# Level scores of an HGRN2 chunk: full-width matmuls replaced by matmuls at the array's four quadrants

## The chip, the cores and the metric

One NeuronCore of one Trainium2 chip. The metric is device time in microseconds of one execution of the whole layer; smaller is better. A core has TensorE (matmuls, with a separate stream of weight loads), VectorE, ScalarE, GpSimd (POOL in the profile) and SyncE (SP, which issues most transfers); each works through its own list of instructions in order and waits where data are missing.

## What is computed

One layer of a hybrid decoder for 256 tokens of width 2048: one wide input projection, three token mixers (a gated linear recurrence, a sliding-window attention, a short convolution), projections, a gated merge, an output projection and a layer norm. The change touches the recurrence alone, whose intra-chunk scores are

```
b = cumsum(log f)                               # per head and channel
diff = b[t] - b[s]
decay = exp(where(causal, diff, -inf))
scores[t, s] = sum_k q[t, k] * k[s, k] * decay[t, s, k]
out[t] = sum_s scores[t, s] * v[s]
```

There are 8 heads with 128 channels each.

## The kernel before

The large matrix products (input projection, branch projections, output projection) take nearly all the time. They are `gemm` calls: weights come in granules of 1 MB (`load_granule`), and each half of a granule is split by `split_w` into a rounded part `hi` (ScalarE, L111) and a rest `lo` (VectorE, L112), so that products in a short float format keep float32 accuracy. `rows` (L140 to L142) and `columns` (L147 to L150) issue the matmuls into one of four `acc` banks. `total` (L188, L189) and others empty the banks. Four buffers each of `hi` and `lo` let the splits run ahead of TensorE.

The recurrence, the attention and the transposes run in the shadow of these products. They are generators in the list `tasks`: after each half granule `gemm` calls `pump()`, which runs the first task up to its next `yield`. So TensorE's list holds the main products with small groups of the tasks' matmuls in between. A scheduler of the framework then fixes the order of instructions on each engine, by its own priorities.

`hgrn(hf, ...)` handles four heads; it runs twice (`hf` 0 and 1). It doesn't form the decay for each pair of tokens. It works in levels h = 1, 2, 4, ..., 128: at level h, the 256 tokens fall into blocks of 2h, and the scores of the upper half of a block (queries) against its lower half (keys) are one product, with the decay split at the boundary between the halves. For each level VectorE and ScalarE make `qc` (queries times `eu`, L346 and L348) and `kk`, a buffer of `kp` (keys times `el`, L347 and L350; two buffers in turn), and carry the prefix and suffix sums on (L352, L353, in `PS`). A product then goes into a PSUM bank `lev`, and its valid part into `st`, which holds the scores of four heads and two chunks of 128 tokens, keys on partitions.

- Levels 1 and 2 use VectorE products summed by a matmul with ones (`near`).
- Levels 4, 8 and 16: for each of 4 heads and 2 chunks one float32 matmul (L385) with 128 key columns as weights against 64 query columns. This gives the scores of all 128 keys with all 64 upper-half queries, of which only the blocks on the diagonal are wanted. One `copy_predicated` on VectorE (L389) moves those into `st`, chosen by a byte mask that stands in `C["mask"]` from column `FAR` on, 64 columns a level.
- Levels 32 and 64 compute only the diagonal blocks (L375), with weights of h columns at partitions 2hi to 2hi + h of the output, and ScalarE copies them (L380). At level 32 these are two places, output partitions 0 to 31 and 64 to 95; at level 64 one.
- Level 128 is one matmul a head (L392, copy L395).

After the levels come the products with the values (L405, L406), the norm and the transposes.

The float32 matmuls of the levels show two records each in the profile, and two weight loads.

Of the kernel before, what the change touches and what calls it, by code (L numbers as in the profile page):

```python
# [16 lines left out]
P = 128  # L17
# [15 lines left out]
EYE, NEAR, FAR, MASKS = 0, {1: 128, 2: 192}, 320, 512  # L33
# [15 lines left out]
def hybrid_kernel(ctx, tc, a, out):  # L49
    nc = tc.nc  # L50
# [16 lines left out]
    def t4(shape, name, dt=F32):  # L67
        return w4.tile(shape, dt, tag="w4", name=name)

    def t2(shape, name, dt=F32):  # L70
        return w4.tile(shape, dt, tag="w2", name=name, bufs=W2)

    def bank(name):
        return bgp.tile([P, NC], F32, tag="bg", name=name)
# [207 lines left out]
    def hgrn(hf, fk, q, v, gate):  # L282
# [20 lines left out]
        def near(e, dst, mask):  # L303

            hi, lo = t2([P, 512], "nh", F32R), t2([P, 512], "nl", F32R)
            nc.scalar.copy(out=hi, in_=e)
            nc.vector.tensor_sub(out=lo, in0=e, in1=f32(hi))
            yield
            ps = bank("near")
            nc.tensor.matmul(out=ps, lhsT=C["ones"], rhs=hi, start=True, stop=False)  # L310
            nc.tensor.matmul(out=ps, lhsT=C["ones"], rhs=lo, start=False, stop=True)
            r = mask.shape[-1]
            nc.vector.copy_predicated(out=dst, mask=mask, data=ps.rearrange("p (x b r) -> p x b r", x=dst.shape[1], r=r))
# [9 lines left out]
        for n, h in enumerate((1, 2, 4, 8, 16, 32, 64, 128)):  # L323
            nb = T // (2 * h)

            def halves(x, h=h):
                y = x.rearrange("p h t -> p (h t)").rearrange("p (b two r) -> p b two r", two=2, r=h)
                return y[:, :, 0], y[:, :, 1]

            qlo, qup = halves(q)  # L330
            klo, kup = halves(k)
            plo, pup = halves(pre)
            slo, sup = halves(suf)
            flo, fup = halves(f)
            qc = t2([P, 4, P], "qc")
            qv = qc.rearrange("p h t -> p (h t)").rearrange("p (b r) -> p b r", r=h)
            kk = kp[:, n % 2]
            if h == 1:
                nc.vector.tensor_mul(out=qv, in0=qup, in1=fup)
                kv = klo  # L340
            else:
                eu = t2([P, 512], "eu")
                el = t2([P, 512], "el")
                euv = eu.rearrange("p (b r) -> p b r", r=h)
                elv = el.rearrange("p (b r) -> p b r", r=h)
                nc.scalar.activation(out=euv, in_=pup, func=AF.Exp)  # L346
                nc.scalar.activation(out=elv, in_=slo, func=AF.Exp)  # L347
                nc.vector.tensor_mul(out=qv, in0=qup, in1=euv)  # L348
                kv = elv if h == 2 else halves(kk)[0]
                nc.vector.tensor_mul(out=kv, in0=klo, in1=elv)  # L350
            if h < 128:
                nc.vector.tensor_add(out=slo, in0=slo, in1=pup[:, :, h - 1 : h].to_broadcast([P, 4 * nb, h]))  # L352
                nc.vector.tensor_add(out=pup, in0=pup, in1=plo[:, :, h - 1 : h].to_broadcast([P, 4 * nb, h]))  # L353
            yield
            if h < 128:
                b = 64 // h
                dst = st.rearrange("p h t (b two r) -> p (h t) b two r", two=2, r=h)[:, :, :, 1]
            if h <= 2:
                for j in range(h):
                    e = t2([P, 512], "e")  # L360
                    nc.vector.tensor_mul(out=e.rearrange("p (b r) -> p b r", r=h), in0=qv,
                                         in1=kv[:, :, j : j + 1].to_broadcast([P, 4 * nb, h]))
                    yield from near(e, dst, C["mask"][:, NEAR[h] + 64 * j : NEAR[h] + 64 * j + 64]
                         .rearrange("p (a b r) -> p a b r", a=1, r=h).to_broadcast([P, 8, b, h]))
                    yield
                continue
            ps = bank("lev")
            if 32 <= h < 128:

                for hd in range(4):  # L370
                    for t in range(2):
                        for i in range(b):
                            s_ = slice(2 * h * i, 2 * h * i + h)
                            o = (2 * hd + t) * h
                            nc.tensor.matmul(out=ps[s_, o : o + h],  # L375
                                             lhsT=kk[:, hd, t * P + s_.start : t * P + s_.stop],
                                             rhs=qc[:, hd, t * 64 + i * h : t * 64 + i * h + h], start=True, stop=True)
                for i in range(b):
                    s_ = slice(2 * h * i, 2 * h * i + h)
                    nc.scalar.copy(out=dst[s_, :, i], in_=ps[s_, : 8 * h].rearrange("p (x r) -> p x r", x=8))  # L380
            elif h < 128:
                for hd in range(4):
                    for t in range(2):
                        o = (2 * hd + t) * 64
                        nc.tensor.matmul(out=ps[:, o : o + 64], lhsT=kk[:, hd, t * P : t * P + P],  # L385
                                         rhs=qc[:, hd, t * 64 : t * 64 + 64], start=True, stop=True)
                m = (C["mask"][:, FAR + 64 * (n - 2) : FAR + 64 * (n - 1)]
                     .rearrange("p (a b r) -> p a b r", a=1, r=h).to_broadcast([P, 8, b, h]))
                nc.vector.copy_predicated(out=dst, mask=m, data=ps.rearrange("p (x b r) -> p x b r", x=8, r=h))  # L389
            else:  # L390
                for hd in range(4):
                    nc.tensor.matmul(out=ps[:, hd * P : hd * P + P], lhsT=kk[:, hd, 0:P], rhs=qc[:, hd],  # L392
                                     start=True, stop=True)
                s01 = t2([P, 4, P], "s01")
                nc.scalar.copy(out=s01, in_=ps.rearrange("p (h t) -> p h t", h=4))  # L395
            yield
# [3 lines left out]
        for t in range(2):  # L400
            ps = bank("pv")
# [14 lines left out]
        o = t4([P, 2, NC], "oa")  # L416
# [126 lines left out]
    C = {}  # L543
# [5 lines left out]
    ps = bank("warm")  # L549
# [4 lines left out]
    for hf in range(2):  # L554
        v = rows_out(rows512(AI + hf, None if hf else first), "va")
        q = t4([P, 4, T], "qa")
        for u in range(2):
            acc = columns256(AQ + 2 * hf + u)
            qr = t2([P, 2, T], "qr")
            for b in range(2):  # L560
                total(qr[:, b], acc[b])
            swish(q[:, 2 * u : 2 * u + 2], qr, HD**-0.5)
        if hf == 0:
            C.update(constants())
        fk = t8([P, 2, 4, T], "fk")
        for u in range(2):
            forget(hf, u, fk[:, 0, 2 * u : 2 * u + 2], columns256(AFG + 2 * hf + u))
        gate = rows_out(rows512(AG + hf), "ga", silu=True)
        nc.gpsimd.tensor_mul(out=gate, in0=gate,
                             in1=C["gn"][:, hf * NC : hf * NC + NC].rearrange("p (o n) -> p o n", o=1)  # L570
                             .to_broadcast([P, 2, NC]))
        tasks.append(hgrn(hf, fk, q, v, gate))
# [15 lines left out]
    for w in range(2):  # L588
        r = slice(64 * w, 64 * w + 64)
# [34 lines left out]
    for d in range(4):  # L624
        m = t4([P, 2, NC], "merged")
# [166 lines left out]
```

## Time and profile before

| | |
|---|---|
| three runs | 1025.15, 1025.85, 1026.55 us; median 1025.85 |
| the profiled execution | 1026.14 us, span of its instructions 1024.3 us |
| TensorE | busy 1009.3 us (99% of the span), 5214 matmul records |
| VectorE | busy 656.9 us (64%) |
| ScalarE | busy 516.8 us (50%) |
| transfers | 192.60 MB, mean 188 GB/s |

The profile is that of one execution. The table gives busy time of engines; an engine's busy share is an average over stages. The span is the time from the first to the last recorded instruction. Times inside rows are microseconds from the span's start. "PE" is TensorE's matmul stream, "PEld" its weight loads, "PEldq" and "DVEq" waits in the engines' instruction sequencers.

### The profile page before, as it was taken

To read this page: it belongs to the slowest core of one execution; us is meant where nothing else is said; L and a number is where in the kernel's file an instruction comes from. 1 tells how busy PE (TensorE), PEld (TensorE's weight loads), DVE (VectorE), ACT (ScalarE), POOL (GpSimd) and SP (SyncE) were. 2 spreads that over 40 slices of the span, in tenths; PEclk is the share of its full clock that TensorE was granted. 3 is DMA by queue.
4 is the path that set the end of the run, shared out by engine and by line. 5 is a ranking of instruction groups with operands and counts; after the bars stand their busy time and mean duration, and the time that the engine had idled before them with its cause. 6 is when DMAs were issued, how large, how long until landed. Compare 5 with 4: busy or idle time off the path is not lost.

```text
span 1024.3 us, 13046 instructions
## 1 busy us (share of the span) xinstructions
PE 1009.3 (99%) x5214; PEld 855.4 (84%) x5214; DVE 656.9 (64%) x810; ACT 516.8 (50%) x702; POOL 32.4 (3%) x32
## 2 busy tenths in 40 slices
PE   8999999999999999999999999999999999999995
PEld 5888888888988888888888888888888888888885
DVE  6557788689855777777764455545554555545666
ACT  5546577656564665646554434444444434444441
POOL 1000000210010000000000000000000000000003
PEclk9999999999999999999999999999999999999998
DMA  8655545354455545444455555555455556665442
GB/s 324 242 194 177 205 136 180 137 189 144 165 196 182 191 156 200 166 168 144 168 199 203 179 194 205 173 197 205 170 200 202 180 193 237 254 248 193 177 164 83
DMA packets 30253, 192.60 MB, mean 188 GB/s; under 512 B 3776, under 2 KB 4576, under 8 KB 8176
## 3 DMA queue, kind: packets, MB, share of 16 engines
q1 hardware_dynamic: 28368, 184.85, 50.9%
q10 hardware_dynamic: 1152, 4.72, 1.3%
q0 software_dynamic: 672, 2.20, 0.7%
q8 instruction: 41, 0.67, 0.3%
q14 instruction: 20, 0.16, 0.0%
HBM read 189.63 MB, written 2.12 MB: 187 GB/s over the span
## 4 chain that ended last, share of the span: by engine, by line
PE 97%; DMA 1%; DVE 1%; SPq 0%; ACT 0%; issue 0%
PE acc L148 24%; PE acc L142 19%; PE acc L140 19%; PE acc L141 19%; PE acc L147 11%; PE lev L385 1%; DMA raw<-in_w_rows 1%; PE sc L454 1%; PE pvb L497 1%; PE acc L150 1%; PE pT L487 1%; PE pv L406 0%; PE mT L259 0%; PE lev L375 0%; DVE xres L677 0%; DVE xres L675 0%
## 5 line engine op out<-in xcount | busy, mean ns | idle before, releaser
L112 DVE TENSOR_TENSOR lo<-raw,hi 128x1024 fp32r<-128x1024 f32 (+1 forms) x341 | 414.9, 1220 | 291.5 <-ACT hi L111 290.5
L111 ACT CAST hi<-raw 128x1024 fp32r<-128x1024 f32 (+1 forms) x341 | 356.7, 1048 | 388.2 <-PE acc L141 264.2
L148 PE MATMUL acc<-xs,hi 128*128 128x512 f32 x1056 | 371.9, 396 | 0.0
L147 PE MATMUL acc<-xs,lo 128*128 128x256 f32 x990 | 278.4, 281 | 0.0
L148 PEld LDWEIGHTS acc<-xs,hi 128*128 128x128 f32 x1056 | 197.0, 188 | 43.7
L140 PE MATMUL acc<-hi,xs 128*128 128x512 f32 (+1 forms) x544 | 210.5, 387 | 2.3 <-ACT hi L111 2.3
L142 PE MATMUL acc<-lo,xs 128*128 128x512 f32 (+1 forms) x544 | 208.4, 384 | 0.4 <-DVE lo L112 0.3
L141 PE MATMUL acc<-hi,xs 128*128 128x512 f32 (+1 forms) x544 | 208.7, 384 | 0.0
L147 PEld LDWEIGHTS acc<-xs,lo 128*128 128x128 f32 x990 | 186.8, 189 | 2.2
L140 PEld LDWEIGHTS acc<-hi,xs 128*128 128x128 f32 x544 | 102.5, 188 | 24.5 <-ACT hi L111 4.4
L142 PEld LDWEIGHTS acc<-lo,xs 128*128 128x128 f32 x544 | 102.2, 188 | 21.3 <-DVE lo L112 1.2
L141 PEld LDWEIGHTS acc<-hi,xs 128*128 128x128 f32 x544 | 102.6, 189 | 19.8
L188 ACT COPY rest<-acc 128x256 f32<-128x256 f32 x66 | 24.3, 373 | 46.2 <-PE acc L148 45.3
L140 PE MATMUL acc<-hi,m 128*128 128x512 f32 (+1 forms) x120 | 45.2, 376 | 0.0
L142 PE MATMUL acc<-lo,m 128*128 128x512 f32 (+1 forms) x120 | 45.0, 375 | 0.0
L141 PE MATMUL acc<-hi,m 128*128 128x512 f32 (+1 forms) x120 | 45.0, 375 | 0.0
L142 PEld LDWEIGHTS acc<-lo,m 128*128 128x128 f32 x120 | 22.6, 188 | 4.1
L140 PEld LDWEIGHTS acc<-hi,m 128*128 128x128 f32 x120 | 22.6, 188 | 4.0
L141 PEld LDWEIGHTS acc<-hi,m 128*128 128x128 f32 x120 | 22.6, 188 | 4.0
L140 PE MATMUL acc<-hi,oa 128*128 128x512 f32 x64 | 24.9, 389 | 0.0
L141 PE MATMUL acc<-hi,oa 128*128 128x512 f32 x64 | 24.9, 389 | 0.0
L142 PE MATMUL acc<-lo,oa 128*128 128x512 f32 x64 | 24.9, 389 | 0.0
(187 smaller groups left out, 912.1 us busy)
## 6 DMA issues: line engine op xcount, KB each, us to landing
raw<-in_w_cols SPq DMA_DIRECT2D x68, 1024.0 KB, 4.8
raw<-in_w_rows SPq DMA_DIRECT2D x60, 1024.0 KB, 4.7
raw<-in_w_out SPq DMA_DIRECT2D x16, 1024.0 KB, 4.8
raw<-in_w_proj_hgrn SPq DMA_DIRECT2D x8, 1024.0 KB, 4.7
raw<-in_w_proj_attn SPq DMA_DIRECT2D x8, 1024.0 KB, 4.7
raw<-in_w_proj_conv SPq DMA_DIRECT2D x8, 1024.0 KB, 4.7
raw<-in_w_rows SPq DMA_DIRECT2D x7, 512.0 KB, 8.9
bias<-bias_dr POOLq DMA_DIRECT2D x2, 1024.0 KB, 6.1
```

The costliest lines, as they stand in the source:

```text
L111: nc.scalar.copy(out=hi, in_=r)
L112: nc.vector.tensor_sub(out=lo, in0=r, in1=f32(hi))
L140: nc.tensor.matmul(out=acc, lhsT=xk[:, 0, ts], rhs=hi, start=first, stop=False)
L141: nc.tensor.matmul(out=acc, lhsT=xk[:, 1, ts], rhs=hi, start=False, stop=False)
L142: nc.tensor.matmul(out=acc, lhsT=xk[:, 0, ts], rhs=lo, start=False, stop=last)
L147: nc.tensor.matmul(out=acc[:, :T], lhsT=lo, rhs=xk[:, 0], start=False, stop=False)
L148: nc.tensor.matmul(out=acc, lhsT=hi, rhs=xk, start=first, stop=last)
L150: nc.tensor.matmul(out=acc[:, :T], lhsT=lo, rhs=xk[:, 0], start=False, stop=False)
L188: nc.scalar.copy(out=rest[p], in_=acc[p, T:])
L385: nc.tensor.matmul(out=ps[:, o : o + 64], lhsT=kk[:, hd, t * P : t * P + P], rhs=qc[:, hd, t * 64 : t * 64 + 64], start=True, stop=True)
L454: nc.tensor.matmul(out=ps[:, o_ : o_ + 2 * nk], lhsT=q[:, 2 * g + x, m, blk * P : blk * P + P], rhs=kz[n][:, hf, :, 0:nk], start=(i == 0), ...
L487: nc.tensor.transpose(out=ps[:, x * P : x * P + P], in_=s[:, x // 2, x % 2, j * P : j * P + P], identity=C["ident"])
```

## The change

At levels 4, 8 and 16 each 128x64 product is replaced by four products of 32 keys with 16 queries (32 weight columns, 16 moving columns), which lie on the diagonal: keys 32i to 32i + 31 of a chunk and the 16 upper-half queries of the same 32 tokens, i = 0 to 3. The contraction still runs over all 128 channels. The output of product i lies at PSUM partitions 32i to 32i + 31, and all 4 x 2 heads and chunks stand next to each other in 16 columns each, 128 columns in all. The one predicated copy of 128 partitions and 512 columns becomes four of 32 partitions and 128 columns, with the matching piece of the same mask. Arithmetic and result stay the same.

```
-                        o = (2 * hd + t) * 64
-                        nc.tensor.matmul(out=ps[:, o : o + 64], lhsT=kk[:, hd, t * P : t * P + P],
-                                         rhs=qc[:, hd, t * 64 : t * 64 + 64], start=True, stop=True)
-                m = (C["mask"][:, FAR + 64 * (n - 2) : FAR + 64 * (n - 1)]
-                     .rearrange("p (a b r) -> p a b r", a=1, r=h).to_broadcast([P, 8, b, h]))
-                nc.vector.copy_predicated(out=dst, mask=m, data=ps.rearrange("p (x b r) -> p x b r", x=8, r=h))
+                        o = (2 * hd + t) * 16
+                        for i in range(4):
+                            nc.tensor.matmul(out=ps[32 * i : 32 * i + 32, o : o + 16],
+                                             lhsT=kk[:, hd, t * P + 32 * i : t * P + 32 * i + 32],
+                                             rhs=qc[:, hd, t * 64 + 16 * i : t * 64 + 16 * i + 16],
+                                             start=True, stop=True)
+                for i in range(4):
+                    r_ = slice(32 * i, 32 * i + 32)
+                    m = (C["mask"][r_, FAR + 64 * (n - 2) + 16 * i : FAR + 64 * (n - 2) + 16 * i + 16]
+                         .rearrange("p (a b r) -> p a b r", a=1, r=h).to_broadcast([32, 8, 16 // h, h]))
+                    nc.vector.copy_predicated(out=dst[r_, :, 16 // h * i : 16 // h * (i + 1)], mask=m,
+                                              data=ps[r_, : 8 * 16].rearrange("p (x b r) -> p x b r", x=8, r=h))
```

Behind the changed place every line number of the new kernel is higher by 7 (its predicated copy is L395).

TensorE's list at level 4 of the second half (`hf` 1), inside the product of the attention's values; before:

```order
L140 MATMUL acc<-hi,xs_84 128x256
L141 MATMUL acc<-hi,xs_84 128x256
L142 MATMUL acc<-lo,xs_84 128x256
L385 MATMUL lev<-qc,kp 128x64 x8
L140 MATMUL acc<-hi,xs_85 128x256
```

and with the change:

```order
L140 MATMUL acc<-hi,xs_84 128x256
L141 MATMUL acc<-hi,xs_84 128x256
L142 MATMUL acc<-lo,xs_84 128x256
L387 MATMUL lev<-qc,kp 32x16 x32
L140 MATMUL acc<-hi,xs_85 128x256
```

Eight matmuls became 32 between the same neighbours; so it is at the other five places, and the rest of TensorE's list is as before.

VectorE's list at level 8 of the second half; L353 is the second of the two sums that the next level needs, before:

```order
L112 TENSOR_TENSOR lo<-raw,hi 128x1024
L353 TENSOR_TENSOR PS<-PS 128x32x16
L389 COPY_PREDICATED st<-mask,lev 128x64x8
L112 TENSOR_TENSOR lo<-raw,hi 128x1024
L348 TENSOR_TENSOR qc<-qa,eu 128x512
L350 TENSOR_TENSOR kp<-fk,el 128x16x32
```

and with the change:

```order
L112 TENSOR_TENSOR lo<-raw,hi 128x1024
L395 COPY_PREDICATED st<-mask,lev 32x8x2x8 x4
L353 TENSOR_TENSOR PS<-PS 128x32x16
L112 TENSOR_TENSOR lo<-raw,hi 128x1024
L588 TENSOR_TENSOR vb<-acc,vb 128x256
L348 TENSOR_TENSOR qc<-qa,eu 128x512
```

The four copies now stand ahead of L353; at level 16 of the second half they pass L353 and one split in the same way. Elsewhere a few neighbours change places.

## Rows read from the trace of the kernel before

**Rows 1.** The page: busy time, granted clock by slice, the chain that ended last.

```profile
PE 1009.3 (99%) x5214; PEld 855.4 (84%) x5214; DVE 656.9 (64%) x810; ACT 516.8 (50%) x702; POOL 32.4 (3%) x32
...
PEclk9999999999999999999999999999999999999998
...
PE 97%; DMA 1%; DVE 1%; SPq 0%; ACT 0%; issue 0%
```

**Rows 2.** Waits of TensorE: us in total, times, longest; later than 30 us none.

```profile
PE acc L140 <- ACT hi L111: 2.3, 2, 1.8
...
PE acc L142 <- DVE lo L112: 0.3, 1, 0.3
```

**Rows 3.** Line L385: durations in ns (min/median/max), first and last start, shape.

```profile
L385 PEld LDWEIGHTS lev<-qc,kp x96: 188/192/192, 147.3 to 268.3; 128*128 128x128 f32 x96
L385 PE MATMUL lev<-qc,kp x96: 217/275/275, 147.5 to 268.3; 128*128 128x64 f32 x96
```

**Rows 4.** Timeline, TensorE, level 4: start, duration in us, engine, line, operation.

```profile
146.94 0.40 PE L148 MATMUL acc<-xs,hi 128*128 128x512 f32 x1
...
147.29 0.39 PE L148 MATMUL acc<-xs,hi 128*128 128x512 f32 x1
147.52 1.89 PE L385 MATMUL lev<-qc,kp 128*128 128x64 f32 x16
...
149.42 0.40 PE L148 MATMUL acc<-xs,hi 128*128 128x512 f32 x1
```

**Rows 5.** Timeline, TensorE, level 32 with 32 weight columns at two places.

```profile
169.32 0.39 PE L148 MATMUL acc<-xs,hi 128*128 128x512 f32 x1
169.64 0.70 PE L375 MATMUL lev<-qc,kp 128*32 128x32 f32 x32
...
170.49 0.39 PE L148 MATMUL acc<-xs,hi 128*128 128x512 f32 x1
```

**Rows 6.** Line L375 by stretch: length, busy time and records begun (x), clock.

```profile
169.14:169.70 0.56, 0.06 (x3) 0.06 (x5) 1.00 0.00 0
169.14:170.12 0.98, 0.48 (x30) 0.48 (x32) 1.00 0.00 0
280.09:280.69 0.60, 0.10 (x1) 0.10 (x2) 1.00 0.00 0
280.09:281.49 1.40, 0.90 (x15) 0.90 (x16) 1.00 0.00 0
```

**Rows 7.** Timeline, TensorE, level 64 with 64 weight columns at one place.

```profile
280.27 0.39 PE L148 MATMUL acc<-xs,hi 128*128 128x512 f32 x1
280.59 1.15 PE L375 MATMUL lev<-qc,kp 128*64 128x64 f32 x16
...
281.89 0.40 PE L148 MATMUL acc<-xs,hi 128*128 128x512 f32 x1
```

**Rows 8.** Timeline, VectorE, level 4 of the second half.

```profile
253.69 0.70 DVE L389 COPY_PREDICATED st<-mask,lev 128x512 f32<-128x512 uint8 x1
254.29 2.34 DVE L112 TENSOR_TENSOR lo<-raw,hi 128x1024 fp32r<-128x1024 f32 x2
```

**Rows 9.** Timeline, VectorE, eight operations of 128 columns in a row.

```profile
195.57 2.16 DVE L420 SCALAR_TENSOR_TENSOR oa<-pv,rs,ga 128x128 f32<-128x128 f32 x8 [1.79 <-POOL rs L415]
```

**Rows 10.** A stretch of VectorE: length, busy time and instructions, clock, transfers.

```profile
224.36:259.50 35.14, 35.14 (x51) 1.00 0.40 141
```

**Rows 11.** Timeline, TensorE: first use of the split behind the copy.

```profile
256.62 0.28 PE L142 MATMUL acc<-lo,xs 128*128 128x256 f32 x1
```

**Rows 12.** Timeline, VectorE and TensorE, level 4 of the second half.

```profile
244.87 0.69 DVE L350 TENSOR_TENSOR kp<-fk,el 128x512 f32<-128x512 f32 x1
...
251.72 1.90 PE L385 MATMUL lev<-qc,kp 128*128 128x64 f32 x16
```

**Rows 13.** Line L392's wait in TensorE's sequencer, and the stretch from it to L392.

```profile
L392 PEldq EVENT_SEMAPHORE  x1: 51/51/51, 284.2 to 284.2; - x1
...
284.28:287.10 2.82, 2.82 (x18) 2.49 (x17) 1.20 (x1) 1.05 (x1) 0.00 (x0) 1.00 0.84 340
```

## Prediction

> **What bounds the kernel now.** I first read the page's busy times, its slices and its chain: TensorE is busy 99% of the span at full granted clock in all slices but the last, and the chain that ended last runs 97% through it [rows 1]. Then the waits of TensorE over the whole span: apart from its first instruction it waited 2.6 us, for hi and lo halves, all of it before 30 us [rows 2], far from the code that changes. So what shortens a TensorE instruction between 130 and 290 us shortens the kernel, unless VectorE then comes late; what VectorE gains or loses counts only through such a lateness.
>
> Next the line that changes. Six blocks (levels 4, 8, 16 in each of two halves) hold 96 matmul records and 96 weight loads, all 128 columns of weights against 64 moving columns [rows 3]: 8 matmuls per block, float32, two records each. Their price is read from the starts of the neighbours, since matmul ends overlap [rows 4]. From the L148 before the block to the L148 behind it pass 149.42 - 147.29 = 2.13 us; two neighbours without a block stand 147.29 - 146.94 = 0.35 us apart. The block costs 1.78 us, 111 ns a record. Six blocks: 10.7 us, 1% of the span.
>
> **What the new block costs.** It has 32 matmuls, so 64 records, each with 32 columns of weights, 16 moving columns and a quadrant of the output. TensorE's order keeps each block's place between the same neighbours, so nothing else moves there. The nearest rows are those of line L375 for level 32, which already uses 32-column weights at two places of the array. There 169.32 to 170.49 is 1.17 us, less the same 0.35: 0.82 us for 32 records [rows 5]. How this splits into a fixed part and a pace is read by counting the records begun up to two moments: 27 records in 0.42 us, 15.6 ns each; the 64-column weights of level 64, which all go to one place, 14 in 0.80 us, 57 ns [rows 6]. Fixed part: 0.82 - 32 x 0.0156 = 0.32 us; from level 64, whose block costs 1.62 - 0.35 = 1.27 us [rows 7], 1.27 - 16 x 0.057 = 0.36 us. I take 0.34. It is the emptying of the array on both sides of a block with narrower weights (the full-width block shows none).
>
> The pace at four places is not in the trace. *Dear end:* as at two places, 15.6 ns: 64 x 0.0156 + 0.34 = 1.34 us, 0.44 saved. *Cheap end:* the columns loaded set the pace (57 ns for 64 columns at one place, about half that for 32, and half again at 15.6 because two places work side by side), then four places halve it to 7.8 ns: 0.84 us, 0.94 saved. Neither is nearer: the form is the first one's, the number of places the other's double. I take the middle, 11.7 ns: 0.75 + 0.34 = 1.09 us, **0.69 us saved a block, 4.1 us for six**; the ends are 2.6 and 5.6 us.
>
> By the Trainium skill (TensorE: Matmul & The Clock Gate, "Part 3: Packing small matmuls — row/col tiling") matmuls at different tiles start about 4 ns apart, with which the cheap end would hold. No row here shows four places, so it moves nothing in the sum.
>
> **VectorE.** One predicated copy of 512 columns becomes four of 128 columns on 32 partitions. The old one stands 0.60 us ahead of its successor (254.29 - 253.69) [rows 8]. The nearest row for a short one is a run of eight 128-column operations out of the same kind of bank: 2.16 / 8 = 0.27 us each [rows 9]. Four cost 1.08, so 0.48 us more a level, 2.9 us in all; if the length meant nothing it would be 4 x 0.60 - 0.60 = 1.8 us more; below 0.48 only if the fixed part fell too. I take 0.48, since the column count is the same.
>
> What hides it: VectorE makes the lo halves ahead of TensorE. The tightest place I found among the six is the first block of the second half. From 224.36 to 259.50 VectorE has no idle time [rows 10], so it cannot catch up. Behind the copy there stand two lo splits, the first done at about 255.5 (half of 2.34 behind 254.29) [rows 8]; TensorE first needs it at 256.62 [rows 11]. Of this 1.1 us the copies take 0.48 and the faster block 0.69: about 0 left, hence no stall in the sum; with the dear copies and the cheap block, 1.1 - 1.8 - 0.9 = 1.6 us of stall, once. The scores' own inputs have more room: the shortest distance from a level's last product (begun 244.87, 0.69 long) to its block (251.72) is 6.2 us [rows 12].
>
> The order also moves on VectorE: in the second half, at levels 8 and 16, the copies now stand ahead of the addition L353. They wait for the block, and behind them now wait that addition, ScalarE's two exponentials for the next level and two products. The old copy of level 8 itself waited for its block, so the move delays the next level by a microsecond or two, and those 6.2 us cover it. On ScalarE a few casts change places with exponentials; TensorE reaches them later by the same cover. No DMA is added; SP and POOL keep their work. TensorE's program grows by 6 x 48 records with their loads, fetched ahead like the rest: nothing.
>
> **Sum.** The profiled execution took 1026.14 us (span 1024.3 and 1.84 around it); 1026.14 - 4.1 = 1022.0. It stands 0.3 above the median of the runs, 1025.85, so I forecast **1021.8 us**.
>
> **The rivals.**
> *A, the forecast* (0.71): the four places work side by side, 7.8 to 15.6 ns: 1020.2 to 1023.3. For it: the even pace over 32 records, and one place's 57 ns against two places' 15.6.
> *B, handing out instructions becomes the bound* (0.15). A block has 128 instructions. At L392 TensorE's sequencer had passed a wait at 284.2 whose matmul came at 287.1, with 18 matmuls and 17 loads between, edges included [rows 13], so it runs some 33 instructions ahead. The 64 of level 32 therefore had about 16 pairs in store and got 16 more within their 0.5 us, a pair in 32 ns at worst. Then 48 pairs of the new block need up to 48 x 0.032 = 1.54 us, with 0.34 together 1.88: 0.10 dearer than before, 6 x 0.1 = 0.6 us, 1026.5. Better paces give anything between that and A; I put its middle at 1024.8. Against it: the pace of level 32 doesn't slacken behind its first 16 records.
> *C, a floor under the distance of two matmuls* (0.04). With a floor of 25 ns, 64 x 0.025 + 0.34 = 1.94 us, 0.16 dearer, 1026.8. Against it: 15.6 ns [rows 6]. Such a floor, about 25 ns from start to start however small the matmul, is a rule of the Trainium skill (TensorE: Matmul & The Clock Gate, "Wait — 56ns, not 53.3ns?"); by this trace it doesn't hold for narrow weights at two places.
> *D, slower: the places do not work side by side* (0.07). Then each record costs a place's own pace, twice 15.6 = 31.2 ns: 64 x 0.0312 + 0.34 = 2.34 us, 0.56 dearer, 6 x 0.56 = 3.4 us: 1029.2. It decides from (1.78 - 0.34) / 64 = 22.5 ns a record. For it: the places beyond two are untried here, and all matmuls keep the full 128 rows. Against it: two places do run together. The Trainium skill (TensorE: Matmul & The Clock Gate, "What overlaps and what doesn't") says that weight loads overlap with matmuls under way only where the row group differs; by that rule this rival would hold, but level 32, whose row groups are all the same, disagrees with its 15.6 ns.
> *E, VectorE's lateness* (0.03): the 1.6 us stall, 4.1 - 1.6 = 2.5 us faster, 1023.3. That the change does not do what it says is excluded by the order: 32 matmuls of 32x16 stand at each of the six places.
>
> **How the numbers follow.** Runs of this kernel spread by 0.14%, so 0.2%, 2.05 us, is about what can be told. A and E are faster by more than that (0.74), as is 0.02 of B; the rest of B and C lie within (0.17); D is slower (0.07). I move 0.01 from faster to slower for a stall that I have not seen. Faster 0.75, same 0.17, slower 0.08. The range reaches from the cheap end of A (5.6 us, 1020.2, less 0.2 of spread) up through B's middle to just above no change: 1020.0 to 1026.0. A alone: 1020.2 to 1023.3.
>
> **What would show it.** Right: blocks of 64 records with the neighbours about 1.4 us apart instead of 2.13, records 8 to 15 ns apart in sixteens without slackening, TensorE's waits unchanged, VectorE about 2.9 us busier. B would show an even first quarter of each block and then a slower pace; C and D an even pace of 25 or 31 ns; E a TensorE wait for lo near 252 us. The forecast is wrong if a block costs 1.78 us or more, or if waits on TensorE between 130 and 290 us eat the difference.

## The result and the profile after

The changed kernel takes 1020.76 us (median of 4 runs, 1019.59 to 1021.02) against 1026.14 us (4 runs, 1025.15 to 1026.55) beside it: ratio 0.9947, 95% interval 0.9929 to 0.9964. A later set of five runs on another occasion gave 1021.62 us against 1026.37, ratio 0.9953 (0.994 to 0.9965). So 4.8 to 5.4 us are saved. The profiled execution took 1020.65 us, with a span of 1018.9 us.

The page of the changed kernel, its busy times, granted clock, instruction queue and chain:

```profile
PE 1004.3 (99%) x5502; PEld 848.5 (83%) x5502; DVE 659.5 (65%) x828; ACT 516.9 (51%) x702; POOL 32.4 (3%) x32
...
PEclk9999999999999999999999999999999999999998
...
q8 instruction: 43, 0.70, 0.3%
...
PE 94%; DVE 4%; DMA 1%; issue 0%; SPq 0%; ACT 0%
```

Against [rows 1], TensorE has 5.0 us less work in 288 more records (six blocks, 48 more each), VectorE 2.6 us more in 18 more instructions, and 3% of the span have passed from TensorE to VectorE in the chain. The chain in order of time (start, length, what) shows where:

```profile
221.06 0.83 DVE yc L189 x2
...
244.62 1.13 DVE lo L112
251.69 1.24 DVE lo L112
```

From 221 us to 253 us, 3% of the span, it runs through VectorE, and it ends in a lo split. These are TensorE's waits (total, times, longest):

```profile
PE acc L140 <- ACT hi L111: 1.3, 2, 0.7
PE acc L142 <- DVE lo L112: 0.8, 2, 0.5
```

Against [rows 2], one of them is new in kind: 0.5 us of the wait for lo falls at 252.97, far behind the start. The list counts only idle time behind the modelled end of the matmul before; by the starts, shown further down, TensorE lost 0.73 us there. The new block, TensorE's timeline at level 4 of the first half, and all its records by line:

```profile
146.75 0.39 PE L148 MATMUL acc<-xs,hi 128*128 128x512 f32 x1
147.07 0.74 PE L387 MATMUL lev<-qc,kp 128*32 128x16 f32 x64
...
147.96 0.40 PE L148 MATMUL acc<-xs,hi 128*128 128x512 f32 x1
```

```profile
L387 PEld LDWEIGHTS lev<-qc,kp x384: 106/109/113, 147.1 to 262.9; 128*32 128x32 f32 x192
L387 PE MATMUL lev<-qc,kp x384: 182/183/203, 147.1 to 262.9; 128*32 128x16 f32 x192
```

From L148 to L148 pass 1.21 us, less the same 0.35 us: the block costs **0.86 us** where it cost 1.78 [rows 4]. A record's own duration of 183 ns says nothing of this: four places overlap, and the ends are modelled. The starts say it. The same line by stretch: length, busy time and records begun (x), clock.

```profile
146.90:147.20 0.30, 0.13 (x14) 0.13 (x18) 1.00 0.00 0
146.90:147.40 0.50, 0.33 (x38) 0.33 (x40) 1.00 0.00 0
146.90:147.57 0.67, 0.50 (x58) 0.50 (x61) 1.00 0.00 0
```

From 147.20 to 147.40 begin 24 records, 8.3 ns each; in the next 0.17 us 20, 8.5 ns each. Record by record the trace shows two paces inside this: up to about the 36th record the starts come in fours every 31.7 ns, 7.9 ns a record (28 from 147.127 to 147.348); after it they come in twos, 8.3 ns a record (20 from 147.411 to 147.576). So the pace slackens by a twentieth, about 0.01 us a block. The granted clock is 1.00 (2.4 GHz) in all of it, as before.

VectorE's timeline at level 4 of the second half, the place that the prediction called the tightest, and TensorE's wait behind it:

```profile
250.39 1.27 DVE L395 COPY_PREDICATED st<-mask,lev 32x128 f32<-32x128 uint8 x4
251.69 2.36 DVE L112 TENSOR_TENSOR lo<-raw,hi 128x1024 fp32r<-128x1024 f32 x2
```

```profile
252.11 0.28 PE L140 MATMUL acc<-hi,xs 128*128 128x256 f32 x1
252.23 0.28 PE L141 MATMUL acc<-hi,xs 128*128 128x256 f32 x1
252.97 0.38 PE L142 MATMUL acc<-lo,xs 128*128 128x256 f32 x1 [0.46 <-DVE lo L112]
253.20 0.28 PE L140 MATMUL acc<-hi,xs 128*128 128x256 f32 x1
```

The four copies stand 1.30 us ahead of their successor, 0.325 us each; the old one stood 0.60 us ahead [rows 8]. Behind them the first of the two splits is done near 252.9 (half of 2.36 behind 251.69), and TensorE waits for it. Neighbours here start 0.12 us apart (252.11 and 252.23), so from this L141 to the L140 two matmuls later 0.24 us would pass. There pass 253.20 - 252.23 = 0.97: the wait costs 0.73 us, of which the list of waits shows 0.46.

**Where the time came from.** Six blocks at 0.92 us less make 5.5 us; the wait takes 0.7 back; that is 4.8 us. The two profiled executions differ by 1026.14 - 1020.65 = 5.5 us. Of this, 0.5 us was there before any changed instruction ran: the L148 ahead of the first block starts at 147.29 before and at 146.75 after. In the executions below the same instruction starts anywhere from 146.09 to 148.08, because the waits at the start of the span differ from run to run, and in four of them the granted clock also stood at 0.50 (1.2 GHz) for a while behind such a wait. So 0.5 us of the profile's difference is not the change's. From that instruction to the end of the span pass 1024.3 - 147.29 = 877.0 us before and 1018.9 - 146.75 = 872.1 after: 4.9 us. The later set of runs, 4.75 us, fits this too.

### The profile page after: what moved, and what is told of

Same layout as the page of the kernel before. It is cut to its first block, busy times and chain, and to the rows that moved or that the text cites. A ratio compares the mean times of both kernels' runs of the same rounds, so it can differ in the third digit from the quotient of the medians.

```text
span 1018.9 us, 13636 instructions
## 1 busy us (share of the span) xinstructions
PE 1004.3 (99%) x5502; PEld 848.5 (83%) x5502; DVE 659.5 (65%) x828; ACT 516.9 (51%) x702; POOL 32.4 (3%) x32
## 4 chain that ended last, share of the span: by engine, by line
PE 94%; DVE 4%; DMA 1%; issue 0%; SPq 0%; ACT 0%
PE acc L148 23%; PE acc L142 19%; PE acc L140 19%; PE acc L141 19%; PE acc L147 11%; DVE lo L112 1%; PE sc L461 1%; DMA raw<-in_w_rows 1%; PE pvb L504 1%; PE acc L150 1%; PE pT L494 1%; PE pv L413 0%; PE mT L259 0%; PE lev L375 0%; PE lev L387 0%
## 5 line engine op out<-in xcount | busy, mean ns | idle before, releaser
L148 PE MATMUL acc<-xs,hi 128*128 128x512 f32 x1056 | 371.9, 396 | 0.0
L148 PEld LDWEIGHTS acc<-xs,hi 128*128 128x128 f32 x1056 | 197.0, 188 | 43.7
L140 PE MATMUL acc<-hi,xs 128*128 128x512 f32 (+1 forms) x544 | 210.6, 387 | 1.3 <-ACT hi L111 1.3
L142 PE MATMUL acc<-lo,xs 128*128 128x512 f32 (+1 forms) x544 | 208.6, 384 | 0.8 <-DVE lo L112 0.8
L141 PE MATMUL acc<-hi,xs 128*128 128x512 f32 (+1 forms) x544 | 208.6, 383 | 0.0
L140 PEld LDWEIGHTS acc<-hi,xs 128*128 128x128 f32 x544 | 102.5, 188 | 23.9 <-ACT hi L111 3.8
L142 PEld LDWEIGHTS acc<-lo,xs 128*128 128x128 f32 x544 | 102.1, 188 | 22.4 <-DVE lo L112 2.3
L141 PEld LDWEIGHTS acc<-hi,xs 128*128 128x128 f32 x544 | 102.6, 189 | 19.6
L140 PE MATMUL acc<-hi,m 128*128 128x512 f32 (+1 forms) x120 | 45.2, 376 | 0.0
L142 PE MATMUL acc<-lo,m 128*128 128x512 f32 (+1 forms) x120 | 45.0, 375 | 0.0
L141 PE MATMUL acc<-hi,m 128*128 128x512 f32 (+1 forms) x120 | 45.0, 375 | 0.0
L141 PEld LDWEIGHTS acc<-hi,m 128*128 128x128 f32 x120 | 22.6, 188 | 4.0
L140 PEld LDWEIGHTS acc<-hi,m 128*128 128x128 f32 x120 | 22.6, 188 | 4.0
L142 PEld LDWEIGHTS acc<-lo,m 128*128 128x128 f32 x120 | 22.6, 188 | 4.0
L140 PE MATMUL acc<-hi,oa 128*128 128x512 f32 x64 | 24.9, 389 | 0.0
L141 PE MATMUL acc<-hi,oa 128*128 128x512 f32 x64 | 24.9, 389 | 0.0
L142 PE MATMUL acc<-lo,oa 128*128 128x512 f32 x64 | 24.9, 389 | 0.0
## 6 DMA issues: line engine op xcount, KB each, us to landing
raw<-in_w_cols SPq DMA_DIRECT2D x68, 1024.0 KB, 4.8
raw<-in_w_rows SPq DMA_DIRECT2D x60, 1024.0 KB, 4.8
raw<-in_w_out SPq DMA_DIRECT2D x16, 1024.0 KB, 4.8
raw<-in_w_proj_hgrn SPq DMA_DIRECT2D x8, 1024.0 KB, 4.7
raw<-in_w_proj_attn SPq DMA_DIRECT2D x8, 1024.0 KB, 4.8
raw<-in_w_proj_conv SPq DMA_DIRECT2D x8, 1024.0 KB, 4.8
bias<-bias_dr POOLq DMA_DIRECT2D x2, 1024.0 KB, 6.1
```

Of the source, the lines that this page charges most:

```text
L140: nc.tensor.matmul(out=acc, lhsT=xk[:, 0, ts], rhs=hi, start=first, stop=False)
L141: nc.tensor.matmul(out=acc, lhsT=xk[:, 1, ts], rhs=hi, start=False, stop=False)
L142: nc.tensor.matmul(out=acc, lhsT=xk[:, 0, ts], rhs=lo, start=False, stop=last)
L148: nc.tensor.matmul(out=acc, lhsT=hi, rhs=xk, start=first, stop=last)
```

## The experiments

Ten runs were made of nine kernels. The first four ask what sets the pace of the small matmuls, the fifth what the copies cost alone, and the others what the copies and the supply of instructions cost beside fast blocks.

**All small matmuls at one place.** The 32 outputs go to the same quadrant, side by side in its columns, and the copies read them there. The scores of three of the four groups of 32 keys are left out.

```diff
-                            nc.tensor.matmul(out=ps[32 * i : 32 * i + 32, o : o + 16],
+                            nc.tensor.matmul(out=ps[0:32, 128 * i + o : 128 * i + o + 16],
...
-                    r_ = slice(32 * i, 32 * i + 32)
+                    r_ = slice(0, 32)
```

> The same 32 matmuls a block with the same 32 weight and 16 moving columns, but all outputs go to partitions 0 to 31, in 512 columns; the copies read from there, so the scores of the other 96 keys are left out. Theory (places side by side make the pace): each record costs one place's own pace, about 31 ns, so a block costs 64 x 0.031 + 0.34 = 2.3 us instead of the 0.86 of the changed kernel, and the kernel takes about 1020.8 + 6 x 1.45 = 1029.5 us. Rival (narrow weights and few moving columns alone make the pace): 8 ns a record, block 0.86 us, 1020.8 us.

```profile
147.50 0.39 PE L148 MATMUL acc<-xs,hi 128*128 128x512 f32 x1
147.82 2.20 PE L387 MATMUL lev<-qc,kp 128*32 128x16 f32 x64
...
150.17 0.40 PE L148 MATMUL acc<-xs,hi 128*128 128x512 f32 x1
```

TensorE's timeline of that kernel: 2.67 - 0.35 = 2.32 us a block, (2.32 - 0.34) / 64 = 31 ns a record. The kernel takes 1029.43 us, 1.0029 of before (1.0017 to 1.0041): slower, by the same 32 matmuls. So the whole gain rests on the four places working side by side, and rival D's price was right for the case that did not come.

**The same matmuls, place after place.** Only the order in TensorE's list changes: first the eight matmuls of place 0, then those of place 1, and so on.

```diff
-                for hd in range(4):
-                    for t in range(2):
-                        o = (2 * hd + t) * 16
-                        for i in range(4):
+                for i in range(4):
+                    for hd in range(4):
+                        for t in range(2):
+                            o = (2 * hd + t) * 16
```

> The same products at the same four places, but ordered place by place: eight matmuls at one place, then the next place. Theory (only neighbours in the order run side by side): about 31 ns a record, block 2.3 us, the kernel about 1029.5 us, 3 us slower than before the change. Rival (each place has its own queue, the order does not matter): 8 ns a record, block 0.86 us, 1020.8 us; a store of some 33 instructions holds eight matmuls, so something between is also open.

```profile
148.06 0.39 PE L148 MATMUL acc<-xs,hi 128*128 128x512 f32 x1
148.38 1.90 PE L387 MATMUL lev<-qc,kp 128*32 128x16 f32 x64
...
150.43 0.40 PE L148 MATMUL acc<-xs,hi 128*128 128x512 f32 x1
```

2.37 - 0.35 = 2.02 us a block; 1027.51 us, 1.0009 of before (0.9998 to 1.0019). The loops' nesting alone decides between 5 us gained and nothing gained. TensorE does not gather the places from far down its list: only where one place follows another do records of two places overlap, and that is the 0.3 us by which this block is cheaper than that of one place. The starts in the trace show how far it reaches: they keep a rhythm of 31.7 ns at each place, and by this rhythm the first three records of the next place begin before the last three of the old one, at each of the three changes (9 x 0.032 = 0.29 us).

**Two places in turn.** Places 0 and 1 alternate through the whole block, then 2 and 3 (line numbers are higher by one).

```diff
-                for hd in range(4):
...
-                            for i in range(4):
+                for ii in ((0, 1), (2, 3)):
+                    for hd in range(4):
...
+                            for i in ii:
```

> The same 32 matmuls in another order: first all those of places 0 and 1 in turn, then all those of places 2 and 3. Theory: a record's pace is the weight load of one place (31.7 ns) over the number of places that take turns in the list, so 15.8 ns, the dear end of the prediction: a block of 0.34 + 64 x 0.0158 = 1.35 us, 6 x 0.49 = 3.0 us more than the changed kernel, about 1023.7 us. Rival: the number of places in turn is not what counts but that neighbours differ at all; then 8 ns, a block of 0.86 us and the changed kernel's time.

Its small matmuls by stretch (length, busy time and records begun, clock):

```profile
147.20:147.50 0.30, 0.13 (x8) 0.13 (x10) 1.00 0.00 0
147.20:147.70 0.50, 0.33 (x20) 0.33 (x22) 1.00 0.00 0
147.20:147.90 0.70, 0.53 (x38) 0.53 (x40) 1.00 0.00 0
...
147.20:148.00 0.80, 0.63 (x45) 0.63 (x47) 1.00 0.00 0
...
147.20:148.20 1.00, 0.83 (x58) 0.83 (x60) 1.00 0.00 0
```

12 records in the first 0.20 us between two of these moments, 16.7 ns each, and 13 in the last, 15.4 ns: the expected 15.8. Between 147.70 and 147.90 there are 18, 11 ns each: there the pair of places changes and records of all four overlap for a while. For this the block (148.62 - 147.05 - 0.35 = 1.22 us by its L148s) is 0.13 us cheaper than expected, and the kernel took 1022.57 us in its one run where 1023.7 was expected; the rival's 0.86 us is out. One, two and four places in turn: 31, 16 and 8 ns.

**64 moving columns at four places.** Each small matmul takes all 64 queries of its tile, and the old single copy reads the result.

```diff
-                            nc.tensor.matmul(out=ps[32 * i : 32 * i + 32, o : o + 16],
+                            nc.tensor.matmul(out=ps[32 * i : 32 * i + 32, o : o + 64],
...
-                                             rhs=qc[:, hd, t * 64 + 16 * i : t * 64 + 16 * i + 16],
-                                             start=True, stop=True)
+                                             rhs=qc[:, hd, t * 64 : t * 64 + 64], start=True, stop=True)
```

> The four places and their order stay, but every matmul moves all 64 query columns instead of 16, so one predicated copy of 128 partitions and 512 columns serves again, as before the change. Theory (the weight columns set the pace): 8 ns a record, block 0.85 to 0.95 us, VectorE back to 657 us busy, no wait for lo near 253 us (0.5 us in the changed kernel), 1020.0 to 1020.8 us. Rival (the moving columns set it): a quarter of the 57 ns that a record of level 64 costs at one place, 14 ns, block 1.26 us, 1022.7 us.

```profile
146.09 0.39 PE L148 MATMUL acc<-xs,hi 128*128 128x512 f32 x1
146.41 1.10 PE L387 MATMUL lev<-qc,kp 128*32 128x64 f32 x64
...
147.66 0.39 PE L148 MATMUL acc<-xs,hi 128*128 128x512 f32 x1
```

1.57 - 0.35 = 1.22 us a block, (1.22 - 0.34) / 64 = 13.8 ns a record, 55 ns per place; 1022.44 us, 0.9963 (0.9948 to 0.9977). My theory that the weights alone set the pace fell: 64 moving columns are dearer than the load of 32. A place is busy for the longer of the two. With the 57 ns of 64 columns at one place [rows 6] and the 31 ns above, that is a little under 1 ns a column, of weights or moving, for the widths tried here.

**The four copies beside the old matmuls.**

```diff
+                        o = (2 * hd + t) * 64
+                        nc.tensor.matmul(out=ps[:, o : o + 64], lhsT=kk[:, hd, t * P : t * P + P],
+                                         rhs=qc[:, hd, t * 64 : t * 64 + 64], start=True, stop=True)
...
+                                              data=ps[r_].rearrange("p (x c r) -> p x c r", x=8, r=h)[:, :, 16 // h * i : 16 // h * (i + 1)])
```

> The full-width matmuls of the kernel before, with the four short predicated copies of the change. Theory (VectorE is covered): a block costs 1.78 us as before, VectorE is about 3 us busier, 1026.1 us, no difference that can be told from the kernel before. Rival (VectorE's extra work reaches TensorE): up to 6 x 0.65 = 3.9 us more, 1030 us, with waits of TensorE for lo or for the level's inputs.

1026.41 us, 1.0001 of before (0.9992 to 1.0011), with VectorE 660.2 us busy, 3.3 more than before, and no wait of TensorE behind the start of the span. The copies alone cost nothing: with the old blocks TensorE comes late enough. So the copies alone do not make the wait at 252.97; what they add to it beside fast blocks, the next two runs show.

**Pairs of quadrants: 32 moving columns, two copies.** A matmul takes the queries of two quadrants, and two copies of 64 partitions x 256 columns take the place of four.

```diff
-                        o = (2 * hd + t) * 16
+                        o = (2 * hd + t) * 32
...
+                            c = t * 64 + 32 * (i // 2)
...
+                                             rhs=qc[:, hd, c : c + 32], start=True, stop=True)
-                for i in range(4):
-                    r_ = slice(32 * i, 32 * i + 32)
+                for j in range(2):
+                    r_ = slice(64 * j, 64 * j + 64)
```

> Each small matmul takes 32 moving columns, the queries of two quadrants, and two predicated copies of 64 partitions x 256 columns take the place of four of 32 x 128. Theory: the pace of a place is the longer of its weight load (32 columns, 31.7 ns in the run with one place) and its moving columns (56 ns per four records at 64 columns, so 28 ns at 32), so four records still take about 32 ns and a block about 0.86 us as in the changed kernel; two copies cost about 0.36 us each, so VectorE is some 0.5 us a level less busy than in the changed kernel, and TensorE's wait of about 0.5 us for a lo half near 253 us goes: 1020.3 us, up to 0.6 us below the changed kernel. Rival: the moving columns already count between 16 and 32, so a block lies between 0.86 us and the 1.22 us of 64 columns, at about 1.0 us, and the kernel is 0.3 to 0.9 us slower than the changed one: 1021.5 us.

**The changed kernel again, beside it.**

> The changed kernel as it is, beside the version with pairs of quadrants, so that the two are compared on one chip. Theory: 1020.8 us within 0.5, blocks of 0.86 us, and once more a TensorE wait of about half a microsecond for a lo half near 253 us, because it comes from VectorE's four copies. Rival: the wait near 253 us was an accident of one execution; then it is absent here.

Pairs, TensorE's block and VectorE's copies at level 4 of the second half:

```profile
147.25 0.39 PE L148 MATMUL acc<-xs,hi 128*128 128x512 f32 x1
147.56 0.76 PE L388 MATMUL lev<-qc,kp 128*32 128x32 f32 x64
...
148.48 0.40 PE L148 MATMUL acc<-xs,hi 128*128 128x512 f32 x1
```

```profile
250.97 0.87 DVE L395 COPY_PREDICATED st<-mask,lev 64x256 f32<-64x256 uint8 x2
251.87 2.36 DVE L112 TENSOR_TENSOR lo<-raw,hi 128x1024 fp32r<-128x1024 f32 x2
```

The changed kernel again, its waits and the one place:

```profile
PE acc L142 <- DVE lo L112: 0.4, 1, 0.4
```

```profile
253.92 0.39 PE L142 MATMUL acc<-lo,xs 128*128 128x256 f32 x1 [0.43 <-DVE lo L112]
```

And the same place with the pairs:

```profile
252.86 0.28 PE L141 MATMUL acc<-hi,xs 128*128 128x256 f32 x1
253.15 0.39 PE L142 MATMUL acc<-lo,xs 128*128 128x256 f32 x1
253.37 0.28 PE L140 MATMUL acc<-hi,xs 128*128 128x256 f32 x1
```

The block of pairs costs 1.23 - 0.35 = 0.88 us: doubling the moving columns from 16 to 32 is nearly free (0.02 us a block), because the load of 32 columns takes as long. The two copies stand 0.90 us ahead of their successor (0.45 each; I had expected 0.36), 0.4 us less than four. TensorE's wait near 253 us is gone from the list of waits, but not from the starts: from L141 to the L140 behind it pass 253.37 - 252.86 = 0.51 us, 0.27 more than the usual 0.24. In the changed kernel the wait is back at the same instruction, 0.43 us in the list, and by the starts 0.70 (254.15 at the L140, 253.21 at the L141: 0.94). So 0.4 us less of copies shortened the wait by 0.4 us, with blocks that differ by 0.02 us: the copies and the faster blocks make it together. The times are 1020.43 us for the pairs (0.9942, 0.9929 to 0.9956) and 1021.62 us for the changed kernel (0.9953, 0.994 to 0.9965). The direction agrees, but the intervals overlap. From the L148 ahead of the first block to the end of the span both profiles show the same 872.1 us within 0.1 (1019.4 - 147.25 and 1019.8 - 147.71), so the 1.2 us between the medians cannot be put down to the pairs: the shorter wait is there, a gain of the kernel is not shown.

**Every block twice.** The last question: does the pace of 8.3 ns come out of a store of instructions that runs dry?

```diff
-                for hd in range(4):
+                for hd in (0, 1, 2, 3, 0, 1, 2, 3):
```

> Every block of the three levels issues its 32 matmuls twice, 128 records instead of 64, the second pass writing the same scores again. Theory: after the first 36 records or so TensorE's store of instructions is empty and a pair is handed out every 8.3 ns, and this pace lasts: a block of 0.34 + 128 x 0.0082 = 1.39 us, 6 x 0.53 = 3.2 us more than the changed kernel, about 1024.0 us. Rival: the 8.3 ns was still fed from something in store that runs out after a block's 64, and then a pair takes longer, 16 ns or more: a block of 1.9 us or more, 1027 us or more.

```profile
147.20:147.62 0.42, 0.32 (x37) 0.32 (x40) 1.00 0.00 0
...
147.20:148.22 1.02, 0.92 (x109) 0.92 (x112) 1.00 0.00 0
```

From 147.62 to 148.22 begin 72 records: 8.33 ns each, still, behind the first 36. The block costs 148.72 - 146.98 - 0.35 = 1.39 us between its L148s, as expected, so B's slackening stays at 8.3 ns up to 128 records. But the time was 1026.25 us (one run), not 1024.0. TensorE stood still twice, behind the second block and within the sixth:

```profile
156.93 0.50 PE L148 MATMUL acc<-xs,hi 128*128 128x512 f32 x1 [1.09 <-ACT el L347]
```

```profile
268.49 0.24 PE L387 MATMUL lev<-qc,kp 128*32 128x16 f32 x4 [1.29 <-issue]
```

By the L148s around them these two blocks are 1.3 and 1.5 us longer than the other doubled ones. With 3.2 us for the blocks, and without the 0.7 us of the wait for lo, which this run does not have, that is 5.3 us; from the L148 ahead of the first block to the end of the span the kernel takes 1024.5 - 146.98 = 877.5 us, 5.4 more than the changed one. The idle 1.29 us stands four records ahead of the block's end and nothing in the trace's semaphores releases it. So it was tried again, and with blocks of 96 records:

> The doubled blocks once more. In the first run of it TensorE stood still for 1.29 us inside its last block, four records before the block's end, with no releaser in the trace. Theory: the store of instructions ran dry there because the next piece of the program had not arrived, which is tied to a place in the program, so the pause is back within the last block at the same record, 1 us or longer, and the time is 1026.2 us within 1. Rival: an accident of one execution; then no pause and about 1025 us.

> Every block issues heads 0 and 1 a second time: 96 records instead of 64. Theory: the pace of 8.3 ns lasts, a block of 0.33 + 96 x 0.0083 = 1.12 us, 6 x 0.26 = 1.6 us more than the changed kernel; the pieces of the program end elsewhere, so a pause, if there is one, stands at another record: about 1022.4 us without one. Rival: the program's pieces arrive in time for 64 records and too late for more, then a pause of about 1 us stands in one or more of the six blocks here too.

The doubled blocks again, TensorE's timeline:

```profile
267.09 1.24 PE L387 MATMUL lev<-qc,kp 128*32 128x16 f32 x124
269.63 0.24 PE L387 MATMUL lev<-qc,kp 128*32 128x16 f32 x4 [1.30 <-issue]
```

The pause is back at the same record, 1.30 us, and so is the one behind the second block (1.2 us in the list); the time is 1026.05 us, ratio 1.0 (0.9988 to 1.0011). With 96 records:

```profile
147.08 0.39 PE L148 MATMUL acc<-xs,hi 128*128 128x512 f32 x1
147.40 1.00 PE L387 MATMUL lev<-qc,kp 128*32 128x16 f32 x96
...
148.56 0.40 PE L148 MATMUL acc<-xs,hi 128*128 128x512 f32 x1
```

1.48 - 0.35 = 1.13 us a block, (1.13 - 0.86) / 32 = 8.4 ns a record, no pause in any block, and 1022.28 us (0.9963, 0.9948 to 0.9979). The list shows no wait for lo either; by the starts there is one of 0.40 us (from L141 at 253.63 to L140 at 254.27).

A pause that returns at one record is tied to a place in the program. The trace shows which. TensorE's program is moved in pieces by queue q8, 46 of them in the doubled kernel (0.75 MB) for 5886 matmul records and as many loads, 256 records a piece; in the changed kernel they are 43 for 5502 and as many, 256 again. The records begun up to the two pauses (length, matmuls and loads; the other columns are other engines'), and q8's last transfer ahead of each, in the windows 154.6 to 154.7 and 266.1 to 266.3:

```profile
0.00:156.92 156.92, 152.42 (x991) 125.97 (x991) 111.63 (x141) 91.79 (x114) 8.26 (x11) 1.00 0.61 213
0.00:268.48 268.48, 262.69 (x2142) 221.82 (x2142) 207.90 (x284) 162.94 (x221) 20.21 (x21) 1.00 0.55 192
```

```profile
q8 instruction: 1, 0.02, 57.2%
...
q8 instruction: 1, 0.02, 28.3%
```

Between the pauses lie 2 x 1151 = 2302 records and two waits in TensorE's sequencer, 2304 in all, nine pieces of 256: both stand at the same place of a piece. The shares are of 16 engines' time, so the two transfers take 0.92 and 0.91 us; begun at 154.63 and 266.19, they end at 155.54 and 267.10, and TensorE goes on 1.39 us behind each. In the second run it is 1.41 and 1.43 us behind. At no other piece of these two traces, and at none in the other traces, does the record at that place come as early as that; in the changed kernel and with 96 records it comes 3.2 us or more behind its piece. So both pauses are read as a piece of the program that arrives late. The profile's name for the first, ScalarE's el, is not the cause: in the changed kernel the same L148 starts at 154.38, before that el (155.37), with the same order on ScalarE. No run moved the pieces by themselves, so this rests on the traces.

## Why the prediction was right, point by point

- **The bound** was right: TensorE is 99% busy in both, and what its records lost, the kernel lost, but for the one wait.
- **The old block's 1.78 us** was right. In the kernel with the old matmuls and the four copies the two L148s around its first block are again 2.13 us apart.
- **The fixed part, 0.34 us**, was right. Blocks of 64, 96 and 128 records cost 0.86, 1.13 and 1.39 us: 8.3 ns a record, and 0.86 - 64 x 0.0083 = 0.33.
- **The pace was the term that was mis-sized.** I called neither end nearer and took the middle, 11.7 ns; it is (0.86 - 0.34) / 64 = 8.1 ns, the cheap end. The block saved 0.92 us instead of 0.69, six of them 1.4 us more than I took. The reason given for the cheap end was the mechanism: the columns loaded keep a place busy, 31 ns for 32, and places that take turns divide it. The cheap end was an argument from two rows that agree (57 ns for 64 columns at one place, 15.6 for 32 at two), the dear end only the fear that it stops at two places; between a mechanism and its bare interruption the middle is no estimate. The rule of the Trainium skill that I set aside (TensorE: Matmul & The Clock Gate, "Part 3: Packing small matmuls — row/col tiling") had pointed to that end. Its 4 ns no run here shows as a pace: 7.9 ns is the least, and inside a group of four the starts are 6 to 7 ns apart.
- **VectorE**: I took 0.27 us a copy and 0.48 us more a level; at the tightest place a copy is 0.325 and the level 0.70 more, because a short predicated copy out of the bank is dearer than the operation whose row I used [rows 9]. The range (0.48 to 1.8) held it. Over the span its busy time grew by 2.6 us, where 2.9 was expected.
- **The tightest place** was right, but the sum put its wait at nothing. The slack was 1.1 us; the copies take 0.70, the faster block 0.92: -0.5 us, and by the starts TensorE loses 0.7. Rival E's mechanism thus came at under half of its price, inside the forecast, and the sign "TensorE's waits unchanged" did not come. Other experiments bear the sum out, to about 0.2 us: with blocks of 1.13 us it gives -0.25 us, with two places (1.22 us) -0.2 and with the pairs' two copies -0.1, and the starts show losses of 0.40, 0.32 (254.62 - 254.06 - 0.24) and 0.27; with the copies beside the old blocks it gives 0.4 to spare, and there is no loss. Part of what the sum lacks is seen in every one of these traces: L142 starts 0.10 us behind the end of its split.
- **Rivals.** A holds, at its lower edge. B is out at the price it was given: behind the 36th record the pace goes from 7.9 to 8.3 ns, and 96 and 128 records keep that; what sets the 8.3 was not tried. C is out with 8.3 ns. The floor of about 25 ns (the Trainium skill, TensorE: Matmul & The Clock Gate, "Wait — 56ns, not 53.3ns?") does not hold for narrow weights at several places. D is out for the change, but it is what one place gives, 31 ns and a kernel that is slower than before. The rule on row groups (the Trainium skill, TensorE: Matmul & The Clock Gate, "What overlaps and what doesn't") disagrees with the 8.3 ns, reached with all row groups the same. The moved instructions on VectorE and ScalarE delayed no block.
- **The sum** gave 1022.0 us for the profiled execution, which took 1020.65: 1.4 us from the pace, 0.5 from the start of the span, which varies, and 0.1 outside the span, less 0.7 for the wait. That the forecast came within 1.1 us of the median is in part luck: the wait that the sum put at nothing took back half of what the pace gave beyond it.

## What to carry to other kernels

Small matmuls with narrow weights run side by side only if neighbours in the list go to different column places: put the loop over places innermost, and count the pace as the longer of weight columns and moving columns at a place, divided by the places in turn, plus about a third of a microsecond a block. Moving columns up to the number of weight columns were then nearly free (32 against 16, with 32 weight columns); they can make the copies behind fewer and wider, though here that gave no gain that shows. And when TensorE gets faster, look for the place where another engine's lead was smallest: that is where a part of the gain is handed back. Measure such a wait by the starts of neighbours: the profile's list of waits showed 0.46 of 0.73 us, and nothing of waits of 0.27 to 0.40.

## What was not expected

- TensorE does not look far ahead in its list for another place: eight matmuls of one place in a row run at 31 ns a record until a few records before the next place, and the block costs 2.02 us instead of 0.86.
- Load and matmul pairs start every 8.3 ns in the second half of a long block, which is close to where four places in turn would have it anyway (31.7 / 4 = 7.9): more places would probably gain little here, though none were tried.
- Blocks of 128 such records met pauses of 1.3 to 1.5 us at two places of the program, nine pieces of 256 records apart, in both runs at the same records, each ending 1.4 us behind a piece of the program. Many tiny instructions are not quite free, even when their pace holds: the list itself has to arrive.
